# Query, key and value projections in 512-column groups, side transfers on GpSimd's queue, and the first norm spread by repeated columns

## The chip, the cores and the metric

The kernel runs on one core of one Trainium2 chip. Of its engines the text speaks of TensorE (PE in the profile; PEld are its weight loads), VectorE (DVE), ScalarE (ACT), GpSimd (POOL) and SyncE (SP), which issues transfers. The metric is the device time of one execution in microseconds (us). Three runs of the kernel before gave 905.86, 905.96 and 906.26 us; the median is 905.96 us.

## What is computed

One layer of a decoder trunk on 512 tokens of 1024 features, in float32. Cut to what matters:

```python
mod = silu(c) @ w_mod + b_mod                      # six vectors of 1024
h = rms_norm(x, norm_mix) * (1 + scale_m) + shift_m
z = h @ w_in                                       # 1024 -> 7424 columns
qa, ka, va, xr, yr, qc, kc, vc, g_logits = split(z)
o_a = swa_attention(rms_norm(qa), rms_norm(ka), va, sinks, bias_a)   # 8 heads of 64, 2 for k and v
o_b = rg_lru(causal_dwconv(xr)) * gelu(yr)
o_c = moba_attention(rms_norm(qc), rms_norm(kc), vc, bias_c)         # 8 heads
merged = sum(sigmoid(g[i]) * (o_i @ w_branch_i) for i in (a, b, c))
x = x + gate_m * (merged @ w_out)
h = rms_norm(x, norm_ffn) * (1 + scale_f) + shift_f
x = x + gate_f * (gated_conv_mlp(h))               # 1024 -> 2 x 2816 -> 1024
```

## The kernel before, in words

**Products in three passes.** Every large operand is kept as a high part (12 leading bits) and a low part, both in a rounded float32 type, and a product is high x high, high x low and low x high, all summed in PSUM. A weight chunk of 128 x 1024 is loaded into one of three `raw` tiles (`stream_to`), and split into `hi` (a copy on ACT, or by `cast` on DVE) and `lo` (a subtraction on DVE, line 240). PSUM has eight banks of 128 x 512; work tiles are 20 slots of 128 x 512 (two to a `pair`) and 60 rounded slots (`rslot`).

**How the order comes about.** The program records operations with a rough clock. `flush` then gives every engine its own fixed order: of its next few operations it takes the first whose operands are there by that clock. On the chip each engine runs its list in that order, and each waits for what it needs.

**The start.** The eight tiles of x, c and the first weights are loaded on SP's queue. c is spread over all partitions, so that w_mod (transposed) can be multiplied by it and summed along the free axis on DVE (`mod_col`, line 246, a custom instruction of 1024 columns). The squares of x are made on ACT and added on DVE, `token_ssq` sums them over the features on PE, and the reciprocal root `rs` (a number per token) has to come to lie along the free axis on all partitions: `spread_diag` writes `ident * rs` as four diagonal blocks (two on DVE, two on ACT), and a product of ones with these blocks (`spread`) puts them in the bank `rbk`. `norm_in(f)` makes the high and the low part of normed feature block f. Then 24 products of 128 x 512 per feature block fill all eight banks (`zb`): k and v of the sliding window, the first k and q of the block attention, and q of the sliding window. `warm` puts products of ones on PE while it waits.

**After the start** the table `ORDER` sets the order of the projections: `v2 v0` (values of the block attention, two groups), `q1 q2 q3` (its keys and queries, three groups), `x`, `y` (recurrence), `g`, `h` (gates ahead of use), `a`, `b`, `c` (branches). A v or q group has 256 columns, two banks and two weight chunks: with a block of 128 tokens as the stationary operand, 256 columns of weights stream past, 8 feature blocks x 4 token blocks x 3 passes = 96 products per group.

**Side tasks** (norms of q and k, transposes, heads, recurrence) are recorded between the products. `turn_task` transposes k, writes its high and low part on one half of the partitions and has a DMA copy each to the other half, since the score products read both halves. A head first loads its bias tile `T` from DRAM (`dswa`, `dmoba`), which `bias_rows` wrote. Gates made ahead go to DRAM (`dg`) and come back; `mod_task` loads the rest of w_mod, `x_task` loads x again. All these transfers go through `E.dma` (line 264), that is through SP's queue, in line with the weight chunks.

Of the kernel before, what the change touches and what calls it, by code (L numbers as in the profile page):

```python
# [17 lines left out]
S = 512  # L18
# [7 lines left out]
# Columns of the per-feature vectors ("vec" input): feature f of a vector sits at partition f % 128,  # L26
# column f // 128 of its range.
# [8 lines left out]
# Columns of the shape-only constants ("cst" input).  # L36
# [19 lines left out]
ORDER = ("v2 v0 q1 h0 x0 x1 g0 q2 g1 g2 g3 h1 h2- a0 q3- x2 y0 y1 h3- g4 h4 a1- m0- a2 a3 a4- x3- g5- y2 "  # L56
# [4 lines left out]
class Buf:  # L61
    """A tile that is used again and again; Tile orders its uses, the emitter picks the ones that are free."""
# [21 lines left out]
class Emitter:  # L84
    """Emits instructions engine by engine and keeps a rough clock of each engine, so that the tensor engine's
    stream takes up work of the side tasks when its operands are there. The order it picks is one of many right
    ones: Tile puts in every wait."""
# [92 lines left out]
    # instructions  # L180
# [68 lines left out]
    def sums(self, out, a):  # L249
        """out[:, h] = the sum of a[:, h, :]."""  # L250
# [12 lines left out]
    def dma(self, out, in_, kb=256):  # L263
        self._go("dma", kb / 370, [out], [in_], lambda: self.nc.sync.dma_start(out, in_))  # L264
# [3 lines left out]
    # the order of issue  # L268
    def flush(self):
        """Issue what was recorded: every engine takes, of its next few instructions, the first whose operands are  # L270
        there, by the same rough clock. Instructions that touch the same buffer keep their order."""
# [26 lines left out]
        def pe_cost(t, i):  # L298
            """The tensor engine runs at half its clock in a window that follows one with little work."""
# [34 lines left out]
        while left:  # L334
# [7 lines left out]
            free[e] = end[i] = t + c  # L342
            if e == "dma":
# [10 lines left out]
    def cast(self, out, in_):  # L354
        """Copy (rounding to out's type) on whichever of the two engines would be done first."""
# [7 lines left out]
    def scale(self, out, in_, col):  # L363
        """out = in_ * col on whichever of the two engines would be done first."""
# [7 lines left out]
    def split(self, hi, lo, x):  # L372
        """hi + lo = x exactly, hi with the 12 leading bits."""
# [7 lines left out]
    def mm3(self, out, wh, wl, xh, xl, first, last):  # L381
        """out (+)= w.T x in three passes; what is left out is the product of the two low parts, below 2^-24."""
# [4 lines left out]
    # side tasks  # L387
# [34 lines left out]
    def pump(self, limit=LIMIT, force=False):  # L422
        """Take up steps of the side tasks that are ready, the oldest first, up to about limit us of tensor work."""
# [45 lines left out]
def hybrid_trunk_kernel(ctx: ExitStack, tc: tile.TileContext, xT, vec, cvec, cst, chot, rel, wm, w8, wz, wgate, wbr,  # L469
# [45 lines left out]
    c8 = sb.tile([128, 8], F32, name="c8")[:]  # L515
    E.dma(c8, cvec, 4)
    E.dma(CS, cst, 66)
# [15 lines left out]
    def stream_to(n_load, n_split):  # L533
        while Stream.loaded < min(n_load, len(plan)):
            i = Stream.loaded
            src = plan[i]
            E.dma(raws[i % 3][:, :src.shape[-1]], src, 4 * 128 * src.shape[-1] / 1024)
            Stream.loaded += 1
        while Stream.split < min(n_split, len(plan)):
            i = Stream.split  # L540
            n = plan[i].shape[-1]
# [16 lines left out]
    def rsqrt(out, ssq, n, inv):  # L558
        """out = (ssq * inv + eps) ** -0.5: a first guess from the exponent, then three Newton steps."""
# [10 lines left out]
    def token_ssq(bk, sq, c0, nb, first=True, last=True):  # L570
        """Sums of squares over the features, a token per partition, a block of tokens per column."""
# [4 lines left out]
    def rsqrt_sqrt(out, st, ssq, n):  # L576
        """out = (ssq / D + eps) ** -0.5 from its rough square root st, by one Newton step."""
# [39 lines left out]
    E.dma(V[:, NEARLY:], vec[:, NEARLY:], 130)  # L617
    # c on every partition; the sums of squares of x, a token per partition, beside it
# [3 lines left out]
    for i in range(2):  # L622
        dg = E.slot()
        for j in range(4):
            E.ts(blk(dg.ap, j), ident, c8[:, 4 * i + j:4 * i + j + 1], None, OP.mult)
        spread(cb[i], 4, dg.ap)
# [868 lines left out]
```

## Time and profile before

| what | before |
|---|---|
| median of three runs | 905.96 us |
| span of the profiled execution (first to last instruction) | 904.7 us |
| PE busy | 895.8 us, 99% of the span |
| DVE, ACT, POOL busy | 630.1, 475.3, 1.8 us |
| granted clock of PE over the span | 0.998 |
| moved by DMA | 131.70 MB, mean 146 GB/s |

The time of the profiled execution is known by its span, which leaves out what lies before the first and behind the last instruction: the median stands 1.26 us above it. A PE row in the timeline gives the start of the first of its instructions, the time to the end of the last, and their count; consecutive products overlap, so the pace of PE is read from start to start. In the other views "busy" is the time in which an engine had work.

### The profile page before, as it was taken

To read this page: it belongs to the slowest core of one execution; us is meant where nothing else is said; L and a number is where in the kernel's file an instruction comes from. 1 tells how busy PE (TensorE), PEld (TensorE's weight loads), DVE (VectorE), ACT (ScalarE), POOL (GpSimd) and SP (SyncE) were. 2 spreads that over 40 slices of the span, in tenths; PEclk is the share of its full clock that TensorE was granted. 3 is DMA by queue.
4 is the path that set the end of the run, shared out by engine and by line. 5 is a ranking of instruction groups with operands and counts; after the bars stand their busy time and mean duration, and the time that the engine had idled before them with its cause. 6 is when DMAs were issued, how large, how long until landed. Compare 5 with 4: busy or idle time off the path is not lost.

```text
span 904.7 us, 12494 instructions
## 1 busy us (share of the span) xinstructions
PE 895.8 (99%) x4730; PEld 772.0 (85%) x4730; DVE 630.1 (70%) x1138; ACT 475.3 (53%) x763; POOL 1.8 (0%) x15
## 2 busy tenths in 40 slices
PE   7999999999999999999999999999999999999998
PEld 6889989889888888878888999888888888888888
DVE  6989989997876875887676888766656665522321
ACT  5366767985875898732223566544444444321110
POOL 0000000000000000000000000000000000000000
PEclk9999999999999999999999999999999999999999
DMA  8933532442254244586667655333222223333320
GB/s 315 347 119 99 155 99 93 129 163 95 73 172 155 90 140 152 184 275 214 229 226 285 213 173 172 123 101 107 97 93 93 93 97 103 104 116 105 117 82 24
DMA packets 44286, 131.70 MB, mean 146 GB/s; under 512 B 5393, under 2 KB 6937, under 8 KB 44226
## 3 DMA queue, kind: packets, MB, share of 16 engines
q1 hardware_dynamic: 44226, 130.90, 43.2%
q8 instruction: 37, 0.61, 0.3%
q14 instruction: 23, 0.19, 0.1%
HBM read 122.46 MB, written 5.80 MB: 142 GB/s over the span
## 4 chain that ended last, share of the span: by engine, by line
PE 93%; ACT 3%; DVE 2%; issue 1%; DMA 0%; SPq 0%; POOLq 0%; POOL 0%; ACTq 0%
PE bank L187 91%; PE bank L191 2%; ACT pair L213 2%; ACT L213 1%; DMA pair<-in_xT_dram 0%; DVE pair L243 0%; DVE pair L240 0%; DVE pair L246 0%; DVE lo L240 0%; ACT hi L213 0%; ACT rslot L213 0%; DVE rslot L240 0%; DVE pair L258 0%; SPq L264 0%; DVE rslot L243 0%
## 5 line engine op out<-in xcount | busy, mean ns | idle before, releaser
L187 PE MATMUL bank<-rslot,hi 128*128 128x512 f32 (+1 forms) x2332 | 656.8, 367 | 0.4 <-ACT rslot L213 0.4
L187 PEld LDWEIGHTS bank<-rslot,hi 128*128 128x128 f32 x2332 | 419.7, 189 | 70.1 <-ACT rslot L213 0.8
L187 PE MATMUL bank<-rslot,lo 128*128 128x512 f32 (+1 forms) x1166 | 427.0, 367 | 0.0
L240 DVE TENSOR_TENSOR lo<-raw,hi 128x1024 fp32r<-128x1024 f32 (+1 forms) x169 | 197.7, 1171 | 151.7 <-ACT hi L213 150.3
L213 ACT ACTIVATE hi<-raw 128x1024 fp32r<-128x1024 f32 (+1 forms) x153 | 156.6, 1025 | 185.3 <-PE bank L187 164.1
L187 PEld LDWEIGHTS bank<-rslot,lo 128*128 128x128 f32 x1166 | 219.9, 189 | 35.8
L187 PE MATMUL bank<-hi,rslot 128*128 128x256 f32 (+1 forms) x448 | 92.0, 315 | 0.1
L243 DVE SCALAR_TENSOR_TENSOR pair<-bank,V,pair 128x511 f32<-128x511 f32 (+2 forms) x112 | 83.6, 746 | 2.8 <-ACT pair L213 1.1
L187 PEld LDWEIGHTS bank<-hi,rslot 128*128 128x128 f32 x448 | 74.3, 190 | 6.3 <-issue 0.9
L213 ACT ACTIVATE rslot<-pair 128x512 fp32r<-128x512 f32 (+2 forms) x60 | 37.2, 622 | 76.7 <-DVE pair L240 72.6
L246 DVE CUSTOM_DVE_ANT_0 pair<-pair,pair,V 128x1024 f32<-128x1024 f32 x48 | 61.1, 1280 | 11.5 <-DMA pair<-in_wm_dram 11.5
L213 ACT ACTIVATE pair<-bank,V 128x512 f32<-128x512 f32 (+1 forms) x84 | 61.5, 732 | 4.8 <-PE bank L187 4.1
L213 ACT ACTIVATE pair<-bank 128x512 f32<-128x512 f32 (+2 forms) x75 | 43.2, 611 | 39.2 <-PE bank L187 38.6
L187 PE MATMUL bank<-lo,rslot 128*128 128x256 f32 (+1 forms) x224 | 62.5, 315 | 0.0
L213 ACT ACTIVATE pair<-pair 128x512 f32<-128x512 f32 (+1 forms) x62 | 35.2, 572 | 47.1 <-DVE pair L243 45.2
L240 DVE TENSOR_TENSOR rslot<-pair,rslot 128x512 fp32r<-128x512 f32 (+2 forms) x67 | 45.5, 680 | 15.2 <-ACT rslot L213 14.7
L240 DVE TENSOR_TENSOR pair<-pair,pair 128x512 f32<-128x512 f32 (+1 forms) x72 | 45.6, 636 | 12.6 <-ACT pair L213 7.6
L213 ACT ACT_TABLE_LOAD x37 | 47.5, 1283 | 5.2 <-PE bank L187 3.8
L187 PE MATMUL bank<-rslot,rslot 128*128 128x256 f32 (+3 forms) x288 | 48.8, 309 | 0.0
L187 PEld LDWEIGHTS bank<-rslot,rslot 128*128 128x128 f32 x288 | 43.4, 189 | 4.7 <-DVE rslot L240 0.8
L213 ACT ACTIVATE pair<-pair,small 128x256 f32<-128x256 f32 (+3 forms) x78 | 40.4, 529 | 11.3 <-DVE small L234 10.3
L187 PEld LDWEIGHTS bank<-lo,rslot 128*128 128x128 f32 x224 | 42.7, 190 | 2.6
(76 smaller groups left out, 412.5 us busy)
## 6 DMA issues: line engine op xcount, KB each, us to landing
raw<-in_wz_dram SPq DMA_DIRECT2D x50, 512.0 KB, 3.8
raw<-in_wup_dram SPq DMA_DIRECT2D x49, 512.0 KB, 3.3
pair<-in_wm_dram SPq DMA_DIRECT2D x48, 512.0 KB, 5.5
raw<-in_wdn_dram SPq DMA_DIRECT2D x22, 512.0 KB, 3.3
raw<-in_wout_dram SPq DMA_DIRECT2D x16, 512.0 KB, 3.3
pair<-in_xT_dram SPq DMA_DIRECT2D x16, 256.0 KB, 5.4
raw<-in_w_dram SPq DMA_DIRECT2D x8, 512.0 KB, 5.5
raw<-in_wbr_dram SPq DMA_DIRECT2D x16, 256.0 KB, 3.0
```

The costliest lines, as they stand in the source:

```text
L187: self._go("pe", cost, [out], [lhsT, rhs], lambda: self.nc.tensor.matmul(out, lhsT, rhs, start=start, stop=stop), rows=lhsT.shape[0] / 128)
L191: self._go("pe", 0.107, [out], [in_, ident], lambda: self.nc.tensor.transpose(out, in_, ident))
L213: self._go("act", c, outs, ins, lambda: self.nc.scalar.activation(out, in_, func, scale=scale, **kw), "tanh" if func == AF.Tanh else t)
L240: self._dve([out], [a, b], lambda: self.nc.vector.tensor_tensor(out, a, b, op=op))
L243: self._dve([out], [a, s, b], lambda: self.nc.vector.scalar_tensor_tensor(out, a, s, b, op0=op0, op1=op1))
L246: self._dve([out, accum], [a, b, s], lambda: self.nc.vector.tensor_tensor_reduce(out, a, b, 1.0, s, op0, op1, accum_out=accum))
```

## The change

It does six things. (1) The groups v2 and v0 become one group V0, and q1 and q2 one group Q1: 512 columns, four banks, four weight chunks put together from two half chunks each by two DMAs; q3 stays as it is. (2) Every side transfer goes through `E.side` on GpSimd's queue; `flush` reckons 0.9 us of POOL for each. (3) c and rs are spread without diagonal blocks: `spread_cols` repeats a column of them 128 times as the stationary operand, against the identity; rs goes to two banks of two token blocks. (4) Three of the eight squares of x move from ACT to DVE, and the sum of squares is closed in another order. (5) c and the identity are loaded on ACT's queue, and the late part of `vec` and the store of c are issued later. (6) A 1.0 that GpSimd wrote into each recurrence tile is written by DVE.

```diff
-ORDER = ("v2 v0 q1 h0 x0 x1 g0 q2 g1 g2 g3 h1 h2- a0 q3- ...
+ORDER = ("V0 h0 Q1 x0 x1 g0 g1 g2 g3 h1 h2- a0 q3- ...
...
+    def side(self, out, in_, kb=256):
+        self._go("pool", 0.9, [out], [in_], lambda: self.nc.gpsimd.dma_start(out, in_), table=kb / 370)
...
-    E.dma(c8, cvec, 4)
-    E.dma(CS, cst, 66)
+    E.dma(c8, cvec, 4, act=True)
+    E.dma(CS, cst, 66, act=True)
...
+            if isinstance(src, tuple):
+                for g in range(2):
+                    E.dma(raws[i % 3].rearrange("p (k g n) -> p k g n", k=2, g=2)[:, :, g],
+                          src[g].rearrange("p (k n) -> p k n", k=2), 256)
...
+    def spread_cols(bk, cols, nb):
+        for i in range(nb):
+            E.mm(blk(bk.ap, i), cols[:, i:i + 1].to_broadcast([128, 128]), ident, True, True)
...
-    E.act(sq.ap, X[0].ap, AF.Square)
-    for k in range(1, KT):
-        s1 = E.slot()
-        E.act(s1.ap, X[k].ap, AF.Square)
-        if k < KT - 1:
-            E.tt(sq.ap, sq.ap, s1.ap, OP.add)
...
+    sq = [E.slot() for _ in range(4)]
+    for k in range(KT):
+        t = sq[0 if k == 0 else 3 if k == 7 else 1 + k % 2]
+        if k in (0, 2, 7):
+            E.tt(t.ap, X[k].ap, X[k].ap, OP.mult)
+        else:
+            E.act(t.ap, X[k].ap, AF.Square)
...
+        if 0 < k < 6:
+            E.tt(sq[0].ap, sq[0].ap, t.ap, OP.add)
...
+    token_ssq(bk, sq[0].ap, 0, 4, True, False)
+    E.tt(sq[3].ap, sq[3].ap, sq[1].ap, OP.add)
+    warm(2)
+    token_ssq(bk, sq[3].ap, 0, 4, False, True)
...
-    spread_diag(rs, 4, dg.ap)
...
+    rbk, rb = [E.bank(), E.bank()], E.slot()
+    for i in range(2):
+        spread_cols(rbk[i], rs[:, 2 * i:2 * i + 2], 2)
...
-        E.dma(d_swa, b.ap[0:8, 0:384], 12)
+        E.side(d_swa, b.ap[0:8, 0:384], 12)
...
-                E.dma(h.ap[o], h.ap[p], 128)
-                E.dma(l.ap[o], l.ap[p], 128)
+                E.side(h.ap[o], h.ap[p], 128)
+                E.side(l.ap[o], l.ap[p], 128)
...
+        if kind in ("Q", "V", "qk"):
+            wid, nk = (256, 4) if kind == "qk" else (512, 2)
+            n = 512 // wid
+            zs = [E.bank() for _ in range(4 // n)]
+            for c in range(KT // nk):
                 wh, wl = next_chunk()
...
+                    for i in range(4):
+                        o = zs[i // n].ap[:, wid * (i % n):wid * (i % n) + wid]
+                        E.mm(o, blk(Hh[f].r, i), wh[:, ws], f == 0 and i % n == 0, False)
+                        E.mm(o, blk(Hh[f].r, i), wl[:, ws], False, False)
+                        E.mm(o, blk(Hl[f].r, i), wh[:, ws], False, f == KT - 1 and i % n == n - 1)
```

In the whole program PE's list loses 384 products of 256 columns (1364 become 980) and gains 192 of 512 (2998 become 3190). 104 transfers leave SP's list for POOL's.

**DVE at the start, from the reciprocal root on** (`small_160` is rs, `pair_65` the first feature block of x, `bank_139` and `bank_140` hold the spread rs):

```order
-L234 TENSOR_SCALAR pair_73<-CS,small_160 128x128 x2
 L246 ISA pair_71,small_152<-pair_71,pair_69,V 128x1024
 L246 ISA small_152 128x1
-L243 SCALAR_TENSOR_TENSOR pair_65<-pair_65,small_152,bank_139 128x256 x2
-L240 TENSOR_TENSOR lo_149<-raw_143,hi_146 128x1024
+L243 SCALAR_TENSOR_TENSOR pair_65<-pair_65,small_152,bank_139 128x256
+L243 SCALAR_TENSOR_TENSOR pair_65<-pair_65,small_152,bank_140 128x256
 L243 SCALAR_TENSOR_TENSOR rslot_83<-pair_65,small_152,rslot_75 128x256 x2
+L240 TENSOR_TENSOR lo_149<-raw_143,hi_146 128x1024
+L234 TENSOR_SCALAR gq<-V 128x1 x2
```

The diagonal blocks are gone from DVE, the low part of the first block moves ahead of the low part of the weights, and two tiny products (`gq`) move in behind.

**ACT between the first products and the next group** (`hi_148` and `hi_146` are the first and second weight chunk of the values; the pairs and rslots are the copies, squares and value parts of the eight banks). Before, the second chunk is split ahead of the eight banks:

```order
L213 ACTIVATE hi_148<-raw_145 128x1024
L213 ACTIVATE hi_146<-raw_143 128x1024
L213 ACT_TABLE_LOAD
L213 ACTIVATE small_165<-small_164 128x8
L213 ACTIVATE pair_71<-bank_140 128x512 x2
```

Now behind all of them:

```order
L213 ACTIVATE pair_72<-bank_136 128x512 x2
L213 ACTIVATE rslot_92<-bank_136 128x2x64
L213 ACTIVATE pair_70<-bank_137 128x512 x2
L213 ACTIVATE pair_66<-bank_138 128x512 x2
L213 ACTIVATE pair_68<-bank_139 128x512
L213 ACTIVATE pair_73<-bank_139 128x512
L213 ACTIVATE pair_65<-bank_140 128x512 x2
L213 ACTIVATE hi_146<-raw_143 128x1024
```

The second chunk of the values can so be used only after the last of the eight banks was read.

**POOL from the bias rows on** (`rslot_93` to `rslot_100` are the k copies, `dswa` the bias rows of the sliding window; before, these stood in SP's list with weight chunks among them):

```order
L273 DMA dswa<-pair_69 8x384
L273 DMA dmoba<-pair_69 8x127
L273 DMA dmoba<-pair_69 8x512
L273 DMA rslot_93<-rslot_93 64x512
L273 DMA rslot_95<-rslot_95 64x512
L273 DMA rslot_94<-rslot_94 64x512
L273 DMA rslot_96<-rslot_96 64x512
L273 DMA rslot_97<-rslot_97 64x512
L273 DMA rslot_99<-rslot_99 64x512
L273 DMA rslot_98<-rslot_98 64x512
L273 DMA rslot_100<-rslot_100 64x512
L273 DMA pair_68<-dswa 128x256
```

The first bias tile of a head stands behind three stores and eight copies in one list, in which each waits for its own operands.

## Rows read from the trace of the kernel before

**Rows 1.** The page, part 1: busy time, share of the span, instructions.

```profile
PE 895.8 (99%) x4730; PEld 772.0 (85%) x4730; DVE 630.1 (70%) x1138; ACT 475.3 (53%) x763; POOL 1.8 (0%) x15
```

**Rows 2.** Windows: stretch, length, busy time of each engine, PE clock, DMA share, GB/s.

```profile
0.00:18.40 18.40, 13.09 (x63) 10.76 (x63) 10.87 (x31) 11.06 (x20) 0.44 (x6) 0.91 0.86 304
18.40:24.20 5.80, 5.72 (x27) 4.43 (x26) 5.76 (x10) 2.67 (x5) 0.00 (x0) 1.00 0.96 344
62.50:200.00 137.50, 137.50 (x919) 124.87 (x917) 129.39 (x376) 111.34 (x255) 0.20 (x2) 1.00 0.39 118
```

**Rows 3.** Timeline of PE, steady products of 512 and of 256 columns.

```profile
29.77 3.79 PE L187 MATMUL bank<-hi,rslot 128*128 128x512 f32 x16
...
35.21 3.79 PE L187 MATMUL bank<-hi,rslot 128*128 128x512 f32 x16
...
64.08 0.40 PE L187 MATMUL bank<-hi,rslot 128*128 128x256 f32 x2
...
64.44 0.40 PE L187 MATMUL bank<-hi,rslot 128*128 128x256 f32 x2
```

**Rows 4.** Timeline of PE: the first two feature blocks, and the first scores.

```profile
18.38 3.91 PE L187 MATMUL bank<-hi,rslot 128*128 128x512 f32 x16
...
24.18 3.94 PE L187 MATMUL bank<-hi,rslot 128*128 128x512 f32 x16
...
86.99 0.64 PE L187 MATMUL bank<-rslot,rslot 128*128 128x256 f32 x4
```

**Rows 5.** Timeline of DVE: the start, and the low part of a weight chunk later.

```profile
10.06 1.49 DVE L240 TENSOR_TENSOR pair<-pair,pair 128x512 f32<-128x512 f32 x2
14.49 0.16 DVE L243 SCALAR_TENSOR_TENSOR small<-small,small 128x4 f32<-128x4 f32 x1
14.68 0.48 DVE L234 TENSOR_SCALAR pair<-CS,small 128x128 f32<-128x128 f32 x2
15.08 1.28 DVE L246 CUSTOM_DVE_ANT_0 pair<-pair,pair,V 128x1024 f32<-128x1024 f32 x1
17.30 0.87 DVE L243 SCALAR_TENSOR_TENSOR pair<-pair,small,bank 128x256 f32<-128x256 f32 x2 [0.93 <-PE bank L187]
18.09 1.22 DVE L240 TENSOR_TENSOR lo<-raw,hi 128x1024 fp32r<-128x1024 f32 x1
19.22 0.88 DVE L243 SCALAR_TENSOR_TENSOR rslot<-pair,small,rslot 128x256 fp32r<-128x256 f32 x2
20.02 1.28 DVE L246 CUSTOM_DVE_ANT_0 pair<-pair,pair,V 128x1024 f32<-128x1024 f32 x1
22.62 0.75 DVE L243 SCALAR_TENSOR_TENSOR pair<-pair,small,pair 128x512 f32<-128x512 f32 x1
...
68.87 1.22 DVE L240 TENSOR_TENSOR lo<-raw,hi 128x1024 fp32r<-128x1024 f32 x1
```

**Rows 6.** Timeline of ACT: the start, and the weight chunk behind the eight banks.

```profile
4.31 0.63 ACT L213 ACTIVATE pair<-pair 128x512 f32<-128x512 f32 x1 [0.23 <-DMA pair<-in_xT_dram]
10.70 0.62 ACT L213 ACTIVATE pair<-pair 128x512 f32<-128x512 f32 x1
13.58 0.26 ACT L213 ACTIVATE small<-bank,epsc 128x4 f32<-128x4 f32 x1 [2.26 <-PE bank L187]
17.82 0.91 ACT L213 ACTIVATE rslot<-pair,small 128x256 fp32r<-128x256 f32 x2 [1.43 <-DVE pair L243]
67.61 1.19 ACT L213 ACTIVATE hi<-raw 128x1024 fp32r<-128x1024 f32 x1
```

**Rows 7.** Timeline of SP: loads of x, and the copies of k.

```profile
1.65 3.74 SPq L264 DMA_DIRECT2D pair<-in_xT_dram  x8
...
77.25 8.41 SPq L264 DMA_DIRECT2D rslot<-rslot  x8
```

**Rows 8.** DMA issues: out<-in, engine, count, KB each, median us to landing.

```profile
rslot<-rslot SPq DMA_DIRECT2D x20, 128.0 KB, 2.2
pair<-dswa SPq DMA_DIRECT2D x8, 128.0 KB, 5.4
```

More of the change, by code (lines that the diff above doesn't have):

```diff
@@ L342, in flush @@
             free[e] = end[i] = t + c
+            if e == "pool" and op[5]:
+                moved = max(t + 1.5, moved) + op[5]
+                end[i] = moved + 0.9
             if e == "dma":
@@ L622, in hybrid_trunk_kernel @@
     for i in range(2):
[L623 to L626, printed above, removed]
-        E.drop(dg)
-    bk = E.bank()
-    sq, wb = E.slot(), E.bank()
+        spread_cols(cb[i], c8[:, 4 * i:4 * i + 4], 4)
+    bk, wb = E.bank(), E.bank()
     def warm(n):
@@ L653, in hybrid_trunk_kernel @@
     stream_to(2, 0)
-    E.ts(gq[:, 0:1], v("qa"), 0.125, None, OP.mult)
-    E.ts(gq[:, 1:2], v("qc"), 0.125, None, OP.mult)
+    E.dma(V[:, NEARLY:], vec[:, NEARLY:], 130)
+    d_c = dr.tile([1, D], F32, name="dc")[:]
+    E.dma(d_c, cp[0].whole[0:1, :], 4)
     scs = [small(2) for _ in range(KT)]
@@ L683, in mod_in, with norm_in @@
             load_wm(f + 2, i)
-    def norm_in(f, low=False, rb=rb):
-        for cs in halves if f < 1 else (slice(0, S),):
+    def norm_in(f, low=False):
+        for i, cs in enumerate(halves if f < 1 else (slice(0, S),)):
             if low:
@@ L696, in hybrid_trunk_kernel @@
     Hl = [E.rslot() for _ in range(KT)]
-    norm_in(0, rb=rbk)
+    norm_in(0)
+    norm_in(0, True)
     E.tt(los[0], raws[0], his[0].bitcast(F32), OP.subtract)
     Stream.split = 1
-    norm_in(0, True)
-    E.act(rb.ap, rbk.ap, AF.Copy)
-    E.drop(rbk)
+    for i in range(2):
+        E.act(rb.ap[:, halves[i]], rbk[i].ap[:, 0:256], AF.Copy)
+    E.drop(*rbk)
+    E.ts(gq[:, 0:1], v("qa"), 0.125, None, OP.mult)
+    E.ts(gq[:, 1:2], v("qc"), 0.125, None, OP.mult)
     zb = [[E.bank() for _ in range(4)] for _ in range(2)]
@@ L764, in bias_tile @@
         w = src.shape[1]
-        E.dma(out, bass.AP(tensor=src.tensor, offset=src.offset + h * w, ap=[[1, 128], [1, n]]), n / 2)
+        E.side(out, bass.AP(tensor=src.tensor, offset=src.offset + h * w, ap=[[1, 128], [1, n]]), n / 2)
     def half(u):
@@ L833, in drop_task, with take_v @@
         E.drop(*zn)
[L835 removed]
+    def take_v(env, src, it):
         if "v" not in env:
             env["v"] = [E.rslot(), E.rslot()]
[L839 to L845 removed]
+        o = env["v"][it // 2].r.rearrange("p (i u s d) -> p i u s d", i=2, u=2, s=2)[:, it % 2]
+        E.act(o[:, :, 0], src, AF.Copy)
+        E.tt(o[:, :, 1], src, o[:, :, 0].bitcast(F32), OP.subtract)
     def v_of(env, kb, u):
@@ L986, in hybrid_trunk_kernel @@
             plan.append(wz[26 + 3 * t + "g h".index(kind)])
+        elif kind in ("Q", "V"):
+            a, b = (0, 2) if kind == "Q" else (6, 8)
+            plan.extend(tuple(wz[o + c // 2][:, 512 * (c % 2):512 * (c % 2) + 512] for o in (a, b)) for c in range(4))
         elif kind != "m":
-            plan.extend(wz[col[kind](t) + i] for i in range(2 if kind in ("qk", "vc") else 1))
+            plan.extend(wz[col[kind](t) + i] for i in range(2 if kind == "qk" else 1))
     for hf in range(2):
@@ L1000, in mod_task @@
         c2 = E.pair()
-        E.dma(c2[0].whole, bass.AP(tensor=d_c.tensor, offset=d_c.offset, ap=[[0, 128], [1, D]]), 512)
+        E.side(c2[0].whole, bass.AP(tensor=d_c.tensor, offset=d_c.offset, ap=[[0, 128], [1, D]]), 512)
         raw = []
@@ L1005, in load @@
             raw.append(E.pair())
-            E.dma(raw[i][0].whole, wm[16 + i], 512)
+            E.side(raw[i][0].whole, wm[16 + i], 512)
         load(0)
@@ L1056, in gate_weights @@
         raw, h, l = E.slot(), E.rslot(), E.rslot()
-        E.dma(raw.ap, wgate[s])
+        E.side(raw.ap, wgate[s])
         yield Need(aps=(raw.ap,))
@@ L1109, in lru_task @@
         E.act(th.ap, th.ap, AF.Sqrt, scale=-1.0)
[L1110 removed]
+        E._dve([th.ap[:, 0:1]], [], lambda: nc.vector.memset(th.ap[:, 0:1], 1.0))
         yield Need(aps=(th.ap, ig.ap))
@@ L1156, in branch @@
             g = E.slot()
-            E.dma(g.ap, d_g[b, t])
+            E.side(g.ap, d_g[b, t])
         else:
@@ L1186, in x_task @@
             XR.append(E.slot())
-            E.dma(XR[k].ap, xT[k])
+            E.side(XR[k].ap, xT[k])
     have_v = []
@@ L1204, in hybrid_trunk_kernel @@
             d_g[b, t] = dr.tile([128, S], F32, name=f"dg{b}{t}")[:]
-            E.dma(d_g[b, t], g.ap)
+            E.side(d_g[b, t], g.ap)
             E.drop(g)
@@ L1221, in hybrid_trunk_kernel @@
             continue
-        E.room(4, 6, 2)
-        if kind in ("qk", "vc"):
-            z2 = [E.bank(), E.bank()]
-            for c in range(2):
+        E.room(4, 6, {"Q": 4, "V": 4, "qk": 2}.get(kind, 1))
+        if kind in ("Q", "V", "qk"):
[3 more added lines that the diff above has]
+            for c in range(KT // nk):
                 wh, wl = next_chunk()
-                for k in range(4):
-                    f = 4 * c + k
-                    ws = slice(256 * k, 256 * k + 256)
+                for k in range(nk):
+                    f = nk * c + k
+                    ws = slice(wid * k, wid * k + wid)
```

88 lines of the change are left out of this document (36 added, 52 removed).

## The prediction

> **What bounds the kernel now.** I read the page first: PE is busy in 895.8 of 904.7 us [rows 1], so this kernel is a line of products with little air in it. Busy time alone would not prove that, since overlapping products count as busy; the pace does. In the timeline of PE, 24 products of 512 columns (one feature block; eight of them lie between the two rows shown) take from 29.77 to 35.21, 0.2267 us each, and three products of 256 columns take from 64.08 to 64.44, 0.120 us each [rows 3]. The windows then tell where there is air: in the first 18.4 us PE is busy for 13.1 and runs mostly on filler; from 62.5 to 200 us it is busy for all 137.5 us [rows 2]. So there are two places to win: the work itself, and the time before the dense stream. The first block starts at 18.38, the second at 24.18 [rows 4], which is 5.80 instead of 5.44 us later, and in between DVE is busy for 5.76 of 5.80 us [rows 2]: DVE sets when the second block can start. The other view to read is DVE from 62.5 to 200 us: 129.4 of 137.5 us, 94% [rows 2]. PE is the bound there, but DVE has only 8.1 us to spare, and a change that keeps DVE waiting will be felt.
>
> The sum is made against the span, 904.7 us; the median of the runs, 905.96, is 1.26 above, and I add that back. A difference of 0.2% is 1.8 us, about what a measurement of this kernel can tell from none.
>
> **Wider groups.** 384 products of 256 columns leave and 192 of 512 come. 384 x 0.120 = 46.08 us go, 192 x 0.2267 = 43.53 us come [rows 3]: **-2.55 us** of pure PE work. A product costs some 11 to 13 ns over its columns (0.2267 less half of it is 0.1134, against 0.120), and the change pays that half as often. All of it lies in a stretch where PE has no idle time, so it counts in full unless another engine takes over as the bound. The Trainium skill (TensorE: Matmul & The Clock Gate, section Back-to-back issue gap) gives the gap of warm products as N / 2.4 GHz plus about 2.5 ns. By it a pair of 256 would cost only 2.5 ns more than one of 512, and the term would be -0.5 us. The rows show 13 ns, and the trace decides.
>
> **The start.** Call R the moment at which rs is done: 14.49 + 0.16 = 14.65 [rows 5]. Up to R the change moves several things. Loading c and the identity on ACT's queue lets the loads of x start about two issues earlier than 1.65, some 0.9 us [rows 7]. ACT pays for these issues with the same 0.8 to 0.9 us, so its first square comes hardly earlier than before (4.31) [rows 6]. DVE then has a chain of its own: five additions into one tile, 0.80 us apart as before (10.06 and the next, 1.49 us for two, the second starting 0.80 later) [rows 5], two squares among them, the square of the last block and one more addition. From about 5.4 us on I get 5 x 0.80 for the additions, 0.6 for the square that does not fit between them, and 2 x 0.7 for the last square and addition: 11.4 us, against 11.3 for the last square on ACT before (10.70 + 0.62) [rows 6]. Behind it only half of the token sums are left for PE, and DVE meanwhile does one modulation column of 1.3 us (two of them and the small operations on them take from 20.02 to 22.62 [rows 5]). So the reciprocal root can begin at 12.8; before, ACT's root was done at 13.58 + 0.26 = 13.84 [rows 6], and R came 0.81 later. R is now 13.6, **1.0 us earlier**, between 0 (if ACT is late with its squares) and 2.
>
> From R to the second block DVE does, in the new order: one modulation column 1.30; the norm of two halves 0.80 (two such operations start 0.80 apart, 19.22 to 20.02); a wait of some 0.35 for ACT's high part, which takes about 0.9 us after 17.82 [rows 6]; the low part 0.80; the low part of the weights 1.13 (18.09 to 19.22); two tiny products, some 0.2; two columns 2.60; then norm and ACT up to the first product, 22.62 to 24.18, 1.56 [rows 4, 5]. That is 8.74 us, where it was 24.18 - 14.65 = 9.53. The diagonal blocks (0.48) and the wait of 0.93 for the spread [rows 5] are gone, because a spread of two token blocks follows R at once and is hidden under the modulation column. The second block starts at 13.6 + 8.74 = 22.3 instead of 24.2: **-1.85 us**. PE itself would be ready sooner: its first block starts 1.30 after R plus the 1.08 from 17.30 to 18.38, at 16.0, and ends at 21.4, so about 0.9 us of idle time before the second block is to be expected. That idle time also covers part of what a low clock would cost: before, the granted clock was 0.91 in the mean of the first 18.4 us [rows 2], that is 3.3 us at the lower level (1.2 GHz). If such a stretch falls on the first block now, it ends 1.7 us later at most and 0.8 of the gain is lost. Bounds of this term: -0.8 and -2.7 us.
>
> **The second chunk of the values.** V0 uses a chunk up in 24 x 0.2267 = 5.44 us, before a chunk lasted longer (48 x 0.120 = 5.76), and two of them had been split before the eight banks were read. Now the second is split behind them. In times of the trace of before: the dense stream reaches V0 at 24.18 + 7 x 5.44 = 62.3, wants the second chunk at 67.7 and its low part four products later, 68.6. ACT came to its first weight chunk behind the banks at 67.61 [rows 6], and DVE had its low part at 68.87 + 1.22 = 70.1 [rows 5]. Against this stand a bias product that PE has in between, and four small operations fewer on ACT. I take **+0.4 us**, between 0 and 1.5.
>
> **The transfers on GpSimd.** No row shows a transfer from that queue. The nearest are those of the same shapes on SP: eight copies of k are issued within 8.41 us, mostly waiting for their operands [rows 7]; a copy lands 2.2 us after its issue, a bias tile after 5.4 [rows 8]. The first copy was issued at 77.25 and the first scores that read it started at 86.99 [rows 4, 7], so a copy may land some 7 us later than it did before PE feels it. I take **0** for the whole move, with bounds of 0 and +10 (worked out below). It can hardly gain: PE has no idle time in which it waits for a transfer that the move speeds up. The 1.0 that DVE now writes (eight tiny operations) and the rest of the edits cost nothing that PE sees; on the other side DVE loses some 2 us of small root steps where two norms of 16 columns become one of 32.
>
> Sum: 904.7 - 2.55 - 1.85 + 0.4 = 900.7; with 1.26, **902.0 us**.
>
> **Rivals.** *GpSimd's queue runs late (slower).* If the queue stays with each transfer for the 2.2 us until it lands instead of about 1, the eight copies take 17.6 instead of 8.4 us, and the bias tiles behind them come 9 us late; with eight tiles at 1 us more each it is 17. DVE adds the bias tile to the scores first of all, so it waits, and it has 8.1 us to spare [rows 2]; the rest, some 9 us, PE waits at the first branch that needs the heads: 911 us. It decides from 8 us of lateness on; slower than before it is from 14 on. For it: one list, in order, of 104 transfers. Against it: the 7 us of slack, and that copies and tiles no longer stand behind weight chunks. The Trainium skill speaks for it: SBUF — State Buffer, section SBUF: two separate sides, says that a GpSimd transfer cannot get its descriptors written while VectorE runs a two-port operation, and gives 0.62 us alone and 3.1 beside one; it advises the other queues. No row of before can show it, since POOL moves nothing there.
>
> *DVE becomes the bound from 62.5 to 200 us (no change).* If the heads already come at DVE's pace, shorter groups only make PE wait for them: 902.0 + 2.55 = 904.6. For it: 94%. Against it: PE idles nowhere there now, and DVE's own list gets shorter.
>
> *The start gains little.* With ACT late and the low clock on the first block it gives 0.8 instead of 1.85: 903.1, still faster.
>
> **How the numbers follow.** Forecast 0.66, small start 0.06, DVE as the bound 0.13, queue late 0.15. Faster by over 0.2% are the forecast and most of the small start, 0.72; within 0.2%: 0.14, the DVE case and a queue that is a little late; slower: 0.14. The forecast's own range is 899.9 (start -2.7, no wait at V0, and more luck with small waits) to 904.1. The range of 8 in 10 reaches over the DVE case and the milder half of the late queue: 899.9 to 907.5.
>
> **What would show it.** In the profile after: the products of 512 still 0.227 apart, 980 of 256 left; rs done at about 13.6 and the second block at about 22.3, with an idle PE before it; less than 1 us of waiting at the second chunk of V0; no wait of PE or DVE for a copy or a bias tile. I am wrong if DVE shows waits of several us for bias tiles, if PE stands idle between 62 and 200 us, or if the first block starts as late as 18.

## The result, and the profile after

The changed kernel takes **927.39 us** (median of 4 runs, 926.67 to 929.76) against 906.11 for the kernel before beside it: ratio 1.0235, 95% interval 1.0219 to 1.025. The forecast was 902.0 us with a range up to 907.5. It is slower by 21 us, and the forecast is wrong.

The page and the windows of the kernel after. The columns are those of [rows 1, 2]:

```profile
PE 902.4 (98%) x4556; PEld 767.1 (83%) x4556; DVE 632.2 (68%) x1125; ACT 475.0 (51%) x754; POOL 61.6 (7%) x119
```

```profile
0.00:16.55 16.55, 11.77 (x80) 11.80 (x81) 10.25 (x22) 8.90 (x15) 0.45 (x6) 1.00 0.91 321
62.50:200.00 137.50, 124.42 (x623) 102.16 (x622) 119.02 (x342) 102.06 (x226) 19.79 (x37) 0.94 0.33 99
```

From 62.5 to 200 us PE was busy for all 137.50 us before [rows 2]. Now it is busy for 124.42, and in the mean at 0.94 of its clock. DVE went down too, from 129.39 to 119.02: nothing took over as the bound, everything waits for something. Finer windows of the kernel after tell where:

```profile
80.00:105.00 25.00, 22.97 (x117) 18.73 (x117) 24.46 (x83) 19.52 (x63) 4.30 (x9) 0.93 0.38 102
105.00:150.00 45.00, 43.82 (x245) 37.89 (x244) 35.26 (x108) 25.88 (x57) 1.96 (x4) 1.00 0.27 88
150.00:200.00 50.00, 40.41 (x186) 32.65 (x185) 42.63 (x105) 44.74 (x88) 8.53 (x16) 0.86 0.31 91
...
178.95:184.10 5.15, 0.28 (x2) 0.08 (x1) 2.37 (x7) 5.10 (x15) 0.55 (x1) 0.74 0.14 36
181.45:188.20 6.75, 3.65 (x12) 3.07 (x13) 5.52 (x16) 6.54 (x12) 0.55 (x1) 0.50 0.15 42
```

I work out what a window lost as its length less PE's busy time, plus the missing share of the clock times the length. From 150 to 200 us that is 9.59 + 0.14 x 50 = 16.6 us, from 80 to 105 us 2.03 + 1.75 = 3.8, from 105 to 150 us 1.2. (The expectations below go by the spacing of the single products, which gives about 1 us more at V0: 4.8 for 3.8, and 7.2 for the 6.1 of e10.) The last two rows show both halves of such a loss: PE runs dry at 178.95, and from 181.45 to 188.20 the granted clock is 0.50, 1.2 GHz. So what follows the gap runs at half pace too.

Who PE waited for, in the view of waits from 60 to 330 us (total, times, longest). The kernel before has no such row there:

```profile
PE bank L187 <- ACT rslot L213: 4.9, 1, 4.9
PE bank L187 <- DVE rslot L240: 2.2, 4, 1.2
PE bank L187 <- DVE small L246: 2.0, 1, 2.0
PE bank L191 <- ACT pair L213: 1.9, 1, 1.9
```

All four are steps of the heads: probabilities, their rounded copies, their row maxima. No transfer is among them. The timeline of PE in the kernel after shows what was missing there:

```profile
160.58 0.39 PE L187 MATMUL bank<-rslot,lo 128*128 128x512 f32 x1
160.80 1.37 PE L187 MATMUL bank<-rslot,rslot 128*128 128x512 f32 x8
164.08 0.89 PE L191 MATMUL bank<-CS,pair 128*128 128x128 f32 x4 [1.90 <-ACT pair L213]
...
176.65 2.58 PE L187 MATMUL bank<-rslot,rslot 128*128 128x256 f32 x17 [0.34 <-DVE rslot L240]
184.17 0.58 PE L187 MATMUL bank<-rslot,rslot 128*128 128x256 f32 x1 [4.93 <-ACT rslot L213]
185.13 0.80 PE L187 MATMUL bank<-rslot,rslot 128*128 128x256 f32 x2 [0.38 <-DVE rslot L240]
185.73 0.63 PE L187 MATMUL bank<-rslot,hi 128*128 128x512 f32 x1
```

A product with hi or lo in it belongs to a projection; it needs only a weight chunk and can fill any wait. From 160.80 until 185.73 none is issued: 68 instructions of heads stand in one row in TensorE's list, between g1 and g2, and wherever ACT or DVE is late nothing fills the wait. In the list of the kernel before the longest such row behind 62 us has 27.

Why the row is there can be followed in the program. Before each gate it calls `E.room(2, 2)`, which asks for two free slots and two free rounded slots (rslot), and otherwise takes steps of the heads until they are free. A k and q pair takes six of the 60 rounded slots as soon as it is turned. Q1 delivers two pairs at once, ahead of the x projections, while the heads of the first kind still use many. When g2 comes, none of the 60 is free (all eight banks are), and the program puts 149 instructions, 69 of them TensorE's, ahead of g2. The gate itself uses no rounded slot. In the kernel before the first such piece comes at q3, with 44 TensorE instructions that are not all in one row. One edit is missing from the six of the change: ahead of an x or y projection the program used to ask for two free banks, and now asks for one. It has no part in this: with two, the piece ahead of g2 is the same 149 and 69.

### The profile page after: what moved, and what is told of

Read it like the earlier page. It is cut to its first block, busy times and chain, and to the rows that moved or that the text cites. A ratio compares the mean times of both kernels' runs of the same rounds, so it can differ in the third digit from the quotient of the medians.

```text
span 924.9 us, 12169 instructions
## 1 busy us (share of the span) xinstructions
PE 902.4 (98%) x4556; PEld 767.1 (83%) x4556; DVE 632.2 (68%) x1125; ACT 475.0 (51%) x754; POOL 61.6 (7%) x119
## 4 chain that ended last, share of the span: by engine, by line
PE 88%; ACT 5%; DVE 4%; issue 1%; DMA 0%; ACTq 0%; DVEq 0%
PE bank L187 86%; PE bank L191 2%; ACT pair L213 2%; ACT rslot L213 1%; ACT L213 1%; DVE pair L246 1%; DVE rslot L243 1%; DVE lo L240 0%; DVE rslot L240 0%; DVE pair L243 0%; DVE pair L234 0%; DMA CS<-in_cst_dram 0%; DVE pair L240 0%; ACT hi L213 0%; DVE pair L258 0%
## 5 line engine op out<-in xcount | busy, mean ns | idle before, releaser
L187 PE MATMUL bank<-hi,rslot 128*128 128x512 f32 (+1 forms) x320 | 86.4, 373 | 0.3 <-ACT rslot L213 0.3
L246 DVE CUSTOM_DVE_ANT_0 pair<-pair,pair,V 128x1024 f32<-128x1024 f32 x48 | 61.0, 1279 | 9.9 <-DMA pair<-in_wm_dram 9.0
L187 PEld LDWEIGHTS bank<-hi,rslot 128*128 128x128 f32 x320 | 57.8, 189 | 10.9 <-issue 0.9
L187 PE MATMUL bank<-rslot,rslot 128*128 128x256 f32 (+3 forms) x288 | 55.9, 332 | 10.5 <-ACT rslot L213 4.9
L213 ACT ACTIVATE pair<-bank 128x512 f32<-128x512 f32 (+3 forms) x76 | 43.2, 608 | 42.8 <-PE bank L187 41.8
L187 PEld LDWEIGHTS bank<-rslot,rslot 128*128 128x128 f32 x288 | 46.1, 202 | 18.5 <-ACT rslot L213 5.9
L213 ACT ACTIVATE pair<-pair 128x512 f32<-128x512 f32 (+1 forms) x59 | 33.1, 568 | 45.4 <-DVE pair L243 44.0
L187 PE MATMUL bank<-lo,rslot 128*128 128x512 f32 (+1 forms) x160 | 51.3, 370 | 0.0
L187 PEld LDWEIGHTS bank<-lo,rslot 128*128 128x128 f32 x160 | 30.2, 189 | 4.9 <-DVE lo L240 0.3
```

Of the source, the lines that this page charges most:

```text
L187: self._go("pe", cost, [out], [lhsT, rhs], lambda: self.nc.tensor.matmul(out, lhsT, rhs, start=start, stop=stop), rows=lhsT.shape[0] / 128)
L213: self._go("act", c, outs, ins, lambda: self.nc.scalar.activation(out, in_, func, scale=scale, **kw), "tanh" if func == AF.Tanh else t)
L246: self._dve([out, accum], [a, b, s], lambda: self.nc.vector.tensor_tensor_reduce(out, a, b, 1.0, s, op0, op1, accum_out=accum))
```

## The experiments

All times are medians; ratios are to the kernel before in the same call. Lost time by windows, worked out as above:

| kernel | time, us | ratio (95%) | 80-105 | 105-150 | 150-200 | 200-270 |
|---|---|---|---|---|---|---|
| after | 927.4 | 1.0235 (1.0219-1.025) | 3.8 | 1.2 | 16.6 | 0.7 |
| e1 wide, SyncE | 923.3 | 1.0191 (1.0162-1.022) | 7.3 | 1.5 | 5.8 | 6.2 |
| e2 narrow, GpSimd | 912.3 | 1.0071 (1.0047-1.0095) | 0 | 0 | 2.7 | 1.1 |
| e3 only V0 wide | 914.4 | 1.0091 (1.0062-1.012) | 5.7 | 0 | 0 | 1.1 |
| e4 only Q1 wide | 915.5 | 1.0099 (1.008-1.0118) | 0 | 0.6 | 5.5 | 0 |
| e5 queue only | 906.9 | 1.0007 (0.9997-1.0018) | 0 | 0 | 0 | 0 |
| e6 start only | 905.2 | 0.9986 (0.9975-0.9996) | 0 | 0 | 0 | 0 |
| e7 narrow, q1 q2 together | 909.1 | 1.003 (1.0018-1.0041) | 0 | 0 | 0.1 | 3.2 |
| e10 wide, late turn | 913.4 | 1.008 (1.0062-1.0099) | 6.1 | 1.2 | 0.3 | 0.8 |
| e12 narrow, late drain | 914.7 | 1.0094 (1.0072-1.0117) | 5.6 | 0 | 0.1 | 2.9 |
| e13 two slots less | 925.2 | 1.0208 (1.0184-1.0231) | 0 | 11.1 | 9.7 | 1.3 |
| e16 wide, heads after V0 | 916.3 | 1.0097 (1.0077-1.0116) | 1.2 | 2.2 | 1.0 | 0.2 |

**Which part?** e1 puts the transfers back on SyncE, e2 the groups back to narrow; e3 and e4 widen one group each.

```diff
 def side(self, out, in_, kb=256):                                # e1
-    self._go("pool", 0.9, [out], [in_], ...gpsimd.dma_start...)
+    self.dma(out, in_, kb)
-ORDER = "V0 h0 Q1 x0 x1 g0 g1 ..."
+ORDER = "v2 v0 q1 h0 x0 x1 g0 q2 g1 ..."                         # e2
+ORDER = "V0 q1 h0 x0 x1 g0 q2 g1 ..."                            # e3
+ORDER = "v2 v0 h0 Q1 x0 x1 g0 g1 ..."                            # e4
```

> The changed kernel with its side transfers put back on SyncE's queue, at the planner's price that they had there; wide groups and new start stay. Theory A (the wide groups V0 and Q1 bunch the work that the other engines do for the heads, so TensorE runs dry between 160 and 185 us): still slow, 920 to 932 us, with idle stretches of TensorE after 85 us and the half clock behind them as in the changed kernel. Theory B (the transfers on GpSimd's queue, or the order that its prices give, are the cause): most of the 21 us comes back, 902 to 907 us.

> The changed kernel with the narrow groups and the order of before (v2 v0 q1 h0 x0 x1 g0 q2); transfers on GpSimd's queue and the new start stay. Theory A (wide groups): the loss is gone and the start's 1.6 us stays, 903 to 906 us. Theory B (queue or its prices): still slow, 918 to 930 us.

> Only V0 is wide; q1 and q2 are narrow and stand where they stood before. Theory A with Q1 as the culprit (two heads' k and q ready at one moment, their turning and their scores bunched): fast, 901 to 907 us, with no idle stretch at 160 to 185 us. Theory A with V0 as the culprit (four banks held from 62 us, the loss at 90 us grows into the later one): slow, 918 to 930 us. Theory B: slow as well, as the transfers are still on GpSimd's queue.

> Only Q1 is wide; v2 and v0 are narrow and stand first as before. Theory A with Q1 as the culprit: slow, 915 to 930 us, with TensorE idle at 160 to 185 us. Theory A with V0 as the culprit: fast, 902 to 908 us, and the 4 us that are lost at 90 to 100 us are gone too.

Neither theory has it all. With the transfers on SyncE the wide kernel is still slow, so theory B falls as the main cause; but with narrow groups the kernel is still 6 us over the one before, where theory A wanted it below. Each wide group loses at a place of its own: V0 at 80 to 105 us, Q1 at 150 to 200. The losses don't add up, though: Q1 alone loses 5.5 us there, with V0 beside it 16.6, and the times of e3 and e4 are only 2 and 3 us above e2's.

**The queue and the start by themselves.** e5 keeps the order of every instruction of the kernel before and only lets GpSimd issue the side transfers (112 of them; the 104 of the change is the net growth of POOL's list, from which eight writes of 1.0 are gone); e6 has only the new start. e8 has no edit of the work.

```diff
-self._go("dma", kb / 370, ..., lambda: self.nc.sync.dma_start(out, in_))
+self._go("dma", kb / 370, ..., lambda: self.nc.gpsimd.dma_start(out, in_))    # e5
-SLACK, NEAR, BACKLOG, LIMIT = 1.2, 2, 8, 2
+SLACK, NEAR, BACKLOG, LIMIT = 1.0, 2, 8, 2                                    # e8
```

> The kernel before, with the side transfers issued by GpSimd but reckoned by the planner as before, so that TensorE, VectorE and ScalarE keep every instruction in its old order: the queue by itself. Theory Q (the queue itself delays what waits for its transfers): 908 to 914 us, with stalls of TensorE behind tiles that land late. Theory O (the queue costs nothing; what cost 6 us in the run with narrow groups is the new order that the planner draws up): 904.5 to 907 us.

> The new start alone: narrow groups in the order of before, side transfers on SyncE. The prediction's term, nothing else lost: 903.5 to 905 us (1.6 us less at the second block). Theory O (each edit, this one too, makes the planner draw up another order behind it, and that order can lose several us at 160 to 210 us): anything from 904 to 915 us, with the loss at 160 to 210 us. Theory Q: 903.5 to 905 us.

> A control without any edit of the work: the kernel before with the planner's SLACK at 1.0 instead of 1.2, which changes only the order in which it issues. It says how far the time moves by the planner's order alone. Theory O: 3 us or more away from 906 us, the loss again between 150 and 260 us. Otherwise: within 2 us.

The queue costs nothing: 1.0007. The copies of k land about as soon as on SyncE, the bias tiles of the sliding window sooner; the issues of e5 (KB each, median us to landing), against 2.2 and 5.4 in [rows 8]:

```profile
rslot<-rslot POOLq DMA_DIRECT2D x20, 128.0 KB, 2.4
pair<-dswa POOLq DMA_DIRECT2D x8, 128.0 KB, 3.3
```

The start gains 1.2 us and is the only part that gains (what made them stands further below). The control moved by 2.0 us (908.36; 1.0026, 1.0014 to 1.0037) through nothing but another order. e2 differs from e6 in the queue and in the prices with which the planner reckons it; if the queue is as free there as in e5, its 7 us come from the order that those prices lead to. In that order rows of 39 and 80 instructions of heads stand ahead of h2 and q3, because none and four of the rounded slots are free where two and six are asked for: the same shortage, without a wide group.

**What is it of Q1?** e7 has narrow groups in the wide kernel's order; e10 keeps the wide groups and turns Q1's second pair late; e13 takes two rounded slots away from e6. (e9, the kernel before with 58 rounded slots from start to end, gave no time: its program gets stuck with so few.)

```diff
-ORDER = "V0 h0 Q1 x0 x1 g0 ..."
+ORDER = "v2 v0 h0 q1 q2 x0 x1 g0 ..."                     # e7
+tz2 = E.spawn(drop_task((), (tz, *attn[:6]))) if g else tz       # e10: tasks of the second pair wait for tz2
-    E.room(2, 2)
+    E.room(2, 0)                                          # e10, e13: gates need no rounded slot
+if (kind, t) == ("xr", 0):                                # e13; given back at a0
+    kept = [E.rslot() for _ in range(2)]
```

> The changed kernel with narrow groups in the order of the wide ones (v2 v0 h0 q1 q2 x0 x1 g0): q1 and q2 stand side by side and their heads come free as early as with Q1, but two banks at a time. If what costs is that two heads' k and q come together ahead of the x projections: 915 to 928 us, with the loss at 160 to 190 us. If it is the four banks held and the second pair released only at the end of a 22 us group: 905 to 913 us.

> The changed kernel, with four banks and wide groups, but the turning of Q1's second pair waits for six of the eight heads of the first kind, so that its six rounded slots are taken late, and the gates (g, h) no longer ask for two free rounded slots, which they don't use. The longest piece of heads without projections shrinks from 69 TensorE instructions ahead of g2 to 36 ahead of q3. Theory S: the loss at 160 to 190 us (16.7 us) goes for the most part, V0's loss at 80 to 100 us (4.8 us) stays, 907 to 914 us. Theory K: nothing is changed for the banks, 918 to 930 us.

> The start alone (905.2 us), narrow groups, SyncE's queue; the only edit of weight is that two of the 60 rounded slots are withheld from the x projections to a0 (and the gates don't ask for free ones, which they don't use). The program then puts 76 TensorE instructions of the heads (176 in all) in one piece ahead of q2, where the kernel with all 60 puts none. Theory S (rounded slots): TensorE runs dry between 105 and 150 us, 912 to 924 us. If the number of slots is not what costs: 904 to 908 us.

e13 shows that a shortage of rounded slots is enough. Nothing of the wide groups is in that kernel, and two of 60 buffers cost 20 us against e6 (there the gates' request was never refused, so dropping it changes no instruction's place). Windows of e13:

```profile
105.00:150.00 45.00, 37.98 (x207) 31.23 (x206) 39.93 (x105) 35.35 (x63) 0.00 (x0) 0.91 0.29 88
150.00:200.00 50.00, 46.29 (x283) 41.31 (x283) 39.94 (x116) 41.92 (x105) 0.00 (x0) 0.88 0.22 63
...
142.70:163.20 20.50, 13.59 (x53) 10.23 (x54) 12.56 (x36) 19.49 (x51) 0.00 (x0) 0.52 0.22 65
```

Its rows of 50 and 26 instructions of heads stand ahead of q2, and there PE runs dry; for 20.5 us the clock is at 0.52. And e10 is the reverse: with Q1 as wide as ever and its four banks held, the loss at 150 to 200 us goes from 16.6 to 0.3. It makes two edits at once; counted in the program, each of them alone takes the piece of 69 away (with the late turn alone the largest piece ahead of a gate has 16 of TensorE's, without the gates' request there is none), but neither was run alone. The windows of e10:

```profile
80.00:105.00 25.00, 22.36 (x102) 17.56 (x102) 23.36 (x80) 19.40 (x62) 4.06 (x9) 0.86 0.40 103
...
150.00:200.00 50.00, 49.67 (x260) 41.52 (x259) 41.64 (x109) 48.44 (x101) 9.38 (x17) 1.00 0.45 128
```

e7 fits: its longest rows have 28 instructions of heads (from 177 us, ahead of h2) and 29 (from 248 us), and it loses only 3.2 us, at the second.

**What is it of V0?** The timeline of PE in the kernel after, where V0 ends:

```profile
89.38 0.40 PE L187 MATMUL bank<-hi,rslot 128*128 128x512 f32 x1
89.80 0.68 PE L187 MATMUL bank<-rslot,rslot 128*128 128x256 f32 x4
92.48 3.47 PE L187 MATMUL bank<-rslot,rslot 128*128 128x256 f32 x16 [2.01 <-DVE small L246]
95.75 0.88 PE L187 MATMUL bank<-rslot,hi 128*128 128x512 f32 x2
```

Here 20 scores of the first heads stand in a row between V0 and h0. A score writes a bank that DVE's row maximum of an earlier head has to read first (small, L246); that ends the wait of 2.01 us, and half clock follows. e12 makes the same of narrow groups: v2's banks are read only after v0.

```diff
 elif kind == "vc":                                        # e12, on e6
+    vz.append((t, zs))
-    take_v(...); E.drop(*zs)
+    if len(vz) == 2: take_v(...) and E.drop(*zs) for both
+late = kind in "QV" and c == KT // nk - 1                 # e14, e15: last chunk, one token block after another
+go.done = go.done or kind != "V"                          # e16, on e10: the first heads wait for go
```

> The start alone (905.2 us), with v2 and v0 narrow, but v2's two banks are read out only after v0's products, together with v0's, as V0's four are. If V0's loss at 90 us comes from four banks that are read out together at its end, when VectorE and ScalarE are needed for the first heads: 3 to 6 us lost between 80 and 105 us, 908 to 912 us. If it comes from the wide products or from h0's place: 904.5 to 906.5 us.

> Both groups wide, the second pair's turning late as in the run e10, the transfers on SyncE, and in the last chunk of a wide group the products of one token block follow each other, so that V0's banks are done and read out one by one, 1.36 us apart, and not four at the end. The longest piece of heads without projections is 18 TensorE instructions. If V0's loss is the reading of four banks at once: 0 to 2.5 us lost at 80 to 105 us instead of 7.2, and with the start and the pace of the wide groups 899 to 905 us, below both kernels. If it is anything else of V0: 907 to 913 us.

> As the run before with the transfers and their prices on GpSimd. The planner's other prices lead to another order, with a piece of 56 TensorE instructions of heads ahead of q3 (117 in all). Theory S: at 80 to 105 us as the run before, and 3 to 9 us lost between 170 and 230 us, 904 to 912 us. If the length of the piece does not matter: the same as the run before within 2 us.

> As the run e10 (both groups wide, GpSimd's queue, the second pair turned late), and the first heads may not begin before V0 is through: their first scores then stand among h0's products and not in one row between V0 and h0 (rows of 12 and 26 TensorE instructions of heads at most, for 20 and 44 in e10). If V0's loss is that row, in which nothing fills TensorE while the banks are read: 0 to 2 us lost at 80 to 105 us for 7.2, and 903 to 909 us. If V0 loses by something else (its second chunk, the four banks themselves, however the rest is ordered): 910 to 915 us.

e12 loses 5.6 us at 80 to 105 us without a wide product, by the same row of 20; its timeline of PE:

```profile
91.15 0.28 PE L187 MATMUL bank<-hi,rslot 128*128 128x256 f32 x1
91.28 0.68 PE L187 MATMUL bank<-rslot,rslot 128*128 128x256 f32 x4
93.97 3.36 PE L187 MATMUL bank<-rslot,rslot 128*128 128x256 f32 x16 [2.01 <-DVE small L246]
97.13 0.52 PE L187 MATMUL bank<-hi,rslot 128*128 128x256 f32 x1
```

Its time, 914.7 us for 908 to 912, was missed. Giving the banks back one by one in the last chunk does not help: e14 (912.38 us; 1.0067, 1.0047 to 1.0086) loses 8.1 us there, e15 (914.48; 1.0094, 1.0064 to 1.0124) 4.2. Both expectations were wrong, but they don't clear the reading of the banks: 16 scores still stand in one row in both, and in e14 the longest wait of PE is another one, 3.71 us for the high part of the next weight chunk, which ACT makes. e16 keeps four banks and lets the scores stand among h0's products; the loss goes to 1.2 us and the half clock with it. So what costs there is the row of scores. That they gather in one row because the banks are held until the end of the group is what e12 suggests; it was not separated further. The window of e16:

```profile
80.00:105.00 25.00, 23.76 (x125) 19.40 (x125) 24.06 (x84) 16.95 (x50) 5.54 (x11) 1.00 0.47 119
```

But the time of e16 was missed too, 916.3 us for 903 to 909: 2.2 us are lost at 105 to 150 us, and 3.0 (its PE busy for 266.99 of 270 us) from 330 to 600 us, where the kernel before loses 0.4.

**A version below both kernels?** e11 and e17 join the start with a wide Q1 that is turned late, v2 and v0 narrow, e11 on GpSimd, e17 on SyncE.

> As the run before, with v2 and v0 narrow again. If the losses of V0 and of Q1 are separate and both causes are found: the start's 1.6 us and Q1's share of the pace, 1.3 us, are left as gains, 902 to 905 us, below both kernels. If something else of the wide Q1 or of the transfers costs: 907 to 915 us.

> A candidate below both kernels: the new start, v2 and v0 narrow, Q1 wide with its second pair turned late, the transfers on SyncE with their old prices; the longest row of heads is 42 TensorE instructions ahead of q3, where the kernel before has 27. Start (-1.3 us measured) and Q1's share of the pace (-1.3 us) with nothing lost: 902.5 to 904.5 us. If the row of 42 costs: 905 to 908 us.

Both missed the gain. e11 is at 907.2 us (1.001, 0.9999 to 1.0021), e17 at 917.7 (1.011, 1.0091 to 1.013), with 3.4 us lost at 200 to 270 us and 5.8 from 330 to 600. Every edit draws up a new order for the whole rest of the program, and these orders lose at new places. I did not follow the losses behind 330 us. What is below both kernels is e6, the start alone: 905.2 us, 0.14% below the kernel before.

## Why the prediction was wrong, step by step

- **Wider groups, -2.55 us: here is the failing step.** It is "it counts in full unless another engine takes over as the bound". I looked for an engine, found DVE with 8 us to spare, and priced that at 2.55. What took over was no engine: the rounded slots for Q1 and, as far as the runs tell, the banks for V0, and through them the place at which the program puts the heads. PE had no idle time there before because a projection stood between any two pieces of heads, and I didn't ask what kept it so. Measured by parts: Q1's stretch 16.6 us, of which e10 gives back 16.3; V0's 3.8, of which e16, counted from e10's 6.1, gives back 4.9.

  The pace itself held only where nothing disturbed it: 18 products of Q1 take from 108.20 to 112.28, 0.2267 us each as forecast. The gap between products is thus the 13 ns of the rows and not the 2.5 ns that the Trainium skill gives (TensorE: Matmul & The Clock Gate, section Back-to-back issue gap). But over all neighbouring products of a group (up to 0.36 us from start to start) the mean in the kernel after is 0.232 us in Q1 and 0.240 in V0, where the narrow groups of the kernel before keep 0.120. These small waits, which the busy time doesn't show, come to about 0.5 and 1.0 us, so some 1 us of the 2.55 was left; where they come from wasn't followed, and no run shows the gain in its time.

Products of Q1 in the kernel after:

```profile
108.20 0.62 PE L187 MATMUL bank<-hi,rslot 128*128 128x512 f32 x2
...
112.28 0.62 PE L187 MATMUL bank<-hi,rslot 128*128 128x512 f32 x2
```

- **The start, -1.85 us: the number nearly came, but most of it is the clock's.** Timelines of PE and of DVE in the kernel after:

```profile
16.55 3.91 PE L187 MATMUL bank<-hi,rslot 128*128 128x512 f32 x16
...
22.61 3.92 PE L187 MATMUL bank<-hi,rslot 128*128 128x512 f32 x16 [0.34 <-ACT rslot L213]
```

```profile
14.05 0.16 DVE L243 SCALAR_TENSOR_TENSOR small<-small,small 128x4 f32<-128x4 f32 x1
```

The second block starts at 22.61 instead of 24.18, 1.57 us earlier; I had 22.3. R came at 14.05 + 0.16 = 14.21, not 13.6, since ACT was late, near the lower end that I had named: its first square starts at 5.52 (before 4.31, rows 6), because c lands 3.1 us after its issue on ACT's queue. The way from R to the second block was 8.40 us for 8.74. The low clock that I feared for the first block didn't come (1.00 in the first 16.55 us).

  In the trace of before it did come (0.54 of the clock from 13.20 to 16.60), and that makes most of the 1.57. e8 has the start of before, at full clock; e12 has the new start, at the low one. The window up to the first block and the start of the second block, first of e8, then of e12:

```profile
0.00:17.00 17.00, 10.85 (x63) 8.39 (x63) 10.85 (x31) 11.01 (x20) 0.44 (x6) 1.00 0.88 305
22.80 3.96 PE L187 MATMUL bank<-hi,rslot 128*128 128x512 f32 x16
```

```profile
0.00:18.10 18.10, 13.12 (x79) 12.96 (x80) 10.65 (x22) 9.04 (x16) 0.45 (x6) 0.91 0.90 322
23.95 3.92 PE L187 MATMUL bank<-hi,rslot 128*128 128x512 f32 x16
```

  At full clock the second block so starts at 22.80 with the old start and at 22.34 to 22.61 with the new one, at the low clock at 23.79 (e5) and 24.18 with the old and 23.79 (e4) and 23.95 with the new: 0.5 us at most at like clock, not 1.85. R is at 14.20 in e8 and at 13.94 to 14.21 with the new start, so it hardly moved. The times say the same: nine of ten runs of e6 had a mean clock of 0.999 or more and took 905.0 to 905.2 us; of the 31 of the kernel before beside it eight had, and took 904.5 to 905.4. The 1.2 us between the medians of e6 and before is therefore how often the low clock falls. Why it falls less often with the new start wasn't tried; that this term nearly hit is luck.

- **V0's second chunk, +0.4 us: within its bounds, a little too large.** From 62.5 to 84.8 us PE is busy for 22.02 of 22.30 us, and the 0.28 lie at 79.56, ahead of a transpose. Where the second chunk comes, one product starts 0.1 us late (at 68.68).

- **The transfers, 0 us: right for the queue, wrong for the move.** e5 gives 1.0007. The rival of the late queue fell: behind the start no wait of PE names a transfer, and the bias tiles land in 3.3 us, earlier than the 5.4 before. The sentence of the Trainium skill that spoke for it (SBUF — State Buffer, section SBUF: two separate sides) didn't show here: from 80 to 105 us DVE is busy for 24.46 of 25.00 us, and POOL's 9 transfers there take 4.30 us, 0.5 each, not 3.1; which of DVE's operations there are two-port ones no row tells. But the move also changed the prices in the planner, and I priced only the chip: e2 against e6 puts 7 us on the order that came of it, if the queue is free there too.

- **The rivals.** DVE as the bound is the nearest, and it is wrong in kind: DVE's busy time fell by 10.4 us in the stretch. Of my signs of being wrong one came, PE idle between 62 and 200 us. None of the rivals was a shortage of buffers, and none reached 927. The range was too narrow because every case in it kept the order of the rest of the program as it was; the two counts that would have told (how many steps of heads stand in a row, 27 and then 68) could be read from the order of the two kernels beforehand.

What stays open: adding the losses of the kernel after to the gains (904.7 + 22.3 - 1.6 - 2.6) gives 922.8 for a span of 924.9; the small waits within the wide groups, some 1.5 us, bring it to 924.3. In e16 the same sum gives 909.6 for 912.4, so 2.8 us have no name there. And the length of a row tells where time is lost, not how much: 80 instructions in a row cost e2 less than 68 cost the kernel after.

## What to carry to other kernels

Where a planner or pools decide the order, ask of each wider or merged step which buffers it takes at once and who is refused them then; a pool that is down to zero is a bound like an engine, and its busy time stands in no profile. Before running, count in the order of the new kernel the longest row of work that waits for others, without filler in between, on the engine that must not stop. And change the work, the queue and the planner's prices in separate runs: here the one part that gained, by 1.2 us, was hidden under others that cost 22 together (927.4 for 905.2). Last, before a gain at the start is put down to an edit, compare stretches with the same granted clock.

## What the runs showed of the hardware

The half clock can add as much again to such a loss, or more, or nothing. In e13, PE was busy for 13.59 of 20.5 us and got 0.52 of its clock all that time; in the kernel after, four stretches at 0.50 lie behind its gaps, and from 150 to 200 us the clock took 7.0 us beside 9.6 of idle time. In the 25 us around V0's end e16 had idle time of 1.2 us in smaller pieces and kept the full clock, e10 had 2.6 and lost another 3.5 to the clock; in e2, 2.7 us of idle time from 150 to 200 us left the clock at 1.00. The new start had the full clock in one execution and 0.91 up to the first block in another (e6 and e12). That a bias tile lands sooner from GpSimd's queue than from SyncE's (3.3 for 5.4 us) I had not expected either; the tiles no longer queue behind weight chunks there, but that this is the reason wasn't tried, and a stored gate lands later (3.3 us in e5 for 2.1).
